# Gate and up of small expert tiles as four products at a time, behind branches of TensorE alone

## The chip, the core and the metric

One Trainium2 chip, one core of it. The time is device microseconds (us) of one execution of the whole program, and the median of 3 runs of the kernel before is 933.65 us (931.49 to 934.76). PE is TensorE, with PEld its weight loads; DVE is VectorE, ACT ScalarE, POOL GpSimd, SP SyncE, the engine that issues the weight transfers. A q behind an engine's name (PEldq) is its sequencer, which reads the instructions, takes the branches and hands work on.

## What is computed

A decoder layer for 512 tokens of width 1024: a mixer (an SSD branch and an attention branch), then a mixture of 16 experts, of which each token goes to two. The change touches the experts alone. Their part of the reference, in which `gates` is zero for all experts but the token's two:

```
for e in range(N_EXPERTS):
    hid = jax.nn.silu(t @ w_gate[e]) * (t @ w_up[e])      # 1024 -> 512, twice
    out = out + gates[:, e:e + 1] * (hid @ w_down[e])     # 512 -> 1024
```

With the inputs of the run, the router sends 31, 40, 95, 86, 27, 11, 40, 32, 91, 132, 170, 103, 25, 21, 59 and 61 tokens to the experts 0 to 15 (counted from the reference on these inputs).

## The kernel before

The mixer fills the first 560 us or so; then come the experts, then a closing layer norm. An expert's tokens are worked in tiles of H = 64: tile 0 always, tile 1 if the expert has more than 64 tokens, tile 2 if more than 128 (`tc.If(n_toks[e] > H)`, L1354, and L1356 inside it). That makes 24 tiles here: experts 2, 3, 8 and 11 have two, 9 and 10 three, the other ten one. A branch is taken by every engine for itself, from the expert's token count, which each engine loads into a register.

What a tile does, `body(e, t)`:

- `up` (L1288): gate and up, 8 steps over the width of 1024. A step is two products of 64 tokens by 512 columns; gate stands in the columns 0 to 63 of TensorE's array and up in 64 to 127, so the two run side by side. They fill one PSUM bank, gate in its upper half and up in its lower.
- `hidden` (L1292, L1293): ACT takes silu of the gate half, DVE multiplies it by the up half, into `sg`.
- `hidden_columns` (L1297, L1298): four transposes of `sg` on PE, and a copy to `hidT` by DVE.
- `down` (L1303): the product with `w_down`, from `hidT`. It is called one tile late: body(e, t) multiplies by `w_down` for the tile before it, between its own `up` and its own `hidden_columns`. `add` (L1307, L1308) then scales the result and adds it into the output rows in DRAM.
- `x_columns` (L1181, L1182) transposes the gathered tokens of the next expert; `tile_tokens` (L1156 to L1165) makes the row numbers and gates of the expert after next, and POOL gathers its tokens.

Rules of order: inside a `with in_order((PE, DVE, ACT))` block each of the three engines keeps the order in which the code is written. What lies between blocks is placed by a scheduler, which lets instructions pass a branch: before, the first products of expert e+1's `up` stand ahead of expert e's branch L1354. The weights come through a ring of 18 buffers of 1 MB, three experts deep.

A row of a four-byte product in the lists of order below is two weight loads and two products in the trace, so four instructions; a transpose is one of each.

Of the kernel before, what the change touches and what calls it, by code (L numbers as in the profile page):

```python
# [9 lines left out]
F32 = mybir.dt.float32  # L10
F32R = mybir.dt.float32r
BF16 = mybir.dt.bfloat16
I32 = mybir.dt.int32
# [4 lines left out]
P = 128  # L18
S = 512
D = 1024  # L20
NT = S // P
KT = D // P
FF = 512
NE = 16
# [4 lines left out]
UNIT = 512  # L29
EVAC = 400  # L30
DUE = 8, 4, 4
H = P // 2
INL = 3
MAXO = 10

# [72 lines left out]
def hybrid_layer(ctx: ExitStack, tc: tile.TileContext, A, out):  # L108
    nc = tc.nc

    cp = ctx.enter_context(tc.tile_pool(name="cp", bufs=1))
# [57 lines left out]
    ident = cp.tile([P, P], F32, name="ident")  # L169
# [67 lines left out]
    class Stream:  # L237
# [7 lines left out]
        def add(self, units, loads, parts):  # L245
            for n, part in enumerate(parts):
                self.parts.append((len(self.raws), n == len(parts) - 1) + part)
            self.raws.append((units, loads))
# [96 lines left out]
    class Experts:  # L345
# [18 lines left out]
        def up(self, e, k):  # L364

            assert self.nload >= 6 * e + 4
            return [self.piece(6 * e + 2 * (k // 4) + n)[:, k % 4 * FF:(k % 4 + 1) * FF] for n in range(2)]

        def down(self, e, k):
            assert self.nload >= 6 * e + 6  # L370
            return [self.piece(6 * e + 4 + k // 2)[:, k % 2 * D + n * 512:k % 2 * D + (n + 1) * 512]
                    for n in range(2)]
# [5 lines left out]
    ew = Experts([(wg_all[e], wu_all[e], wd_all[e]) for e in range(NE)], [])  # L378
# [25 lines left out]
    for j in range(4):  # L404
# [14 lines left out]
        for t, sc_ in enumerate((1, 0)):  # L419
            o = 8 * sc_ + 2 * j  # L420
# [142 lines left out]
    for g in range(4):  # L563
# [17 lines left out]
        for c in range(NT):  # L581
            nc.tensor.matmul(pt[:, c * P:(c + 1) * P], Bc.ap[:, c * P:(c + 1) * P], Cc.ap[:, c * P:(c + 1) * P],
                             start=True, stop=True)
# [14 lines left out]
        for c2 in range(2):  # L598
            pt = tr.get()
            for c in (2 * c2, 2 * c2 + 1):  # L600
                for t in range(2):
                    o = (c % 2) * 256 + t * P
# [96 lines left out]
    for j in range(4):  # L699
# [22 lines left out]
        for i in range(NT):  # L722
            w = (i + 1) * P
# [36 lines left out]
        o = FM.alloc(1)  # L760
# [81 lines left out]
    for j in range(8):  # L842
        for y in (ys[j], ya[j]):
            pt = proj(hT, KT)
            t = FM.alloc(1)
# [18 lines left out]
    def rtile(nm, shape, dt=F32):  # L864
        if dt is I32:
            return cp.tile(shape, dt, name=f"rt_{nm}")
        n = 1
        for d in shape[1:]:
            n *= d
        w = n if dt is F32 else -(-n // 2)  # L870
        a = rtc[0][:, rtc[1]:rtc[1] + w]
        if dt is not F32:
            a = a.bitcast(dt)[:, 0:n]
        rtc[1] += -(-w // 2) * 2
        for ax_ in range(len(shape) - 1, 1, -1):
            a = a.rearrange("p (a b) -> p a b", b=shape[ax_]) if ax_ == len(shape) - 1 else \
                a.rearrange("p (a b) c -> p a b c", b=shape[ax_])
        return a
# [8 lines left out]
    half = rtile("half", [P, 1])  # L887
    nc.vector.tensor_scalar(half, pcol, float(H), None, op0=ALU.is_ge)
    nc.vector.tensor_scalar(itb[:, 0:H], itf[:, 0:H], 1.0, None, op0=ALU.add)
    nc.vector.tensor_copy(itb[:, H:P], itb[:, 0:H])  # L890
    itbs = [itb] + [rtile(f"itb{t}", [P, P], BF16) for t in range(1, INL)]
    for t in range(1, INL):
        nc.vector.tensor_scalar(itbs[t], itb, float(t * H), None, op0=ALU.add)
    aux = rtile("aux", [P, NT, NE, 5], BF16)
# [82 lines left out]
    @contextmanager  # L977
    def in_order(engines):

        traced = nc.cur_bb.bb.instructions  # L980
        n, prev = len(traced), {}
        yield
        for ins in traced[n:]:
            if ins.engine in engines:
                if ins.engine in prev:
                    tc.add_manual_dep(ins, prev[ins.engine], mybir.DependencyInfo(
                        mybir.DependencyClass.NoSync, mybir.DependencyReason.DATA), reason="in_order")
                prev[ins.engine] = ins.name
# [60 lines left out]
    ET = mybir.EngineType  # L1049
# [60 lines left out]
    bgu, bys, bhid, bix = (banks[0], banks[1], banks[1]), [banks[2], banks[6]], banks[5], banks[7]  # L1110
    h2d2 = h2d.rearrange("s (h d) -> (s h) d", h=2)
    moed2 = moed.rearrange("s (h d) -> (s h) d", h=2)
    xgs, xTs, sgs, yos, ohs = {}, {}, [], [], []
# [12 lines left out]
    def setup_experts():  # L1126
# [6 lines left out]
        yos.extend(FM.alloc(1).ap for _ in range(2))  # L1133
        hidT.append(FM.alloc(1).v(4, H))
        for _ in range(3):
# [4 lines left out]
        ew.raws.append(xrc[1].ap)  # L1140
        ew.load()

    ixs = [[rtile(f"ix{e}{t}", [P, 1], I32) for t in range(INL)] for e in range(3)]
    gws = [[rtile(f"gw{e}{t}", [P, 1]) for t in range(INL)] for e in range(3)]
    ixl = [rtile(f"ixl{e}", [P, 1], I32) for e in range(2)]
    gwl = [rtile(f"gwl{e}", [P, 1]) for e in range(2)]
    rkx = rtile("rkx", [P, NT])

    def onehots(oh, ranks, slots):
# [3 lines left out]
    def tokens(oh, au, ix, gw, xg, n0=0, n1=5, at=128):  # L1153

        pi = bix[:, at + n0:at + n1]
        nc.tensor.matmul(pi, onesb, bigb[:, n0:n1], start=True, stop=False)  # L1156
        for c in range(NT):
            nc.tensor.matmul(pi, oh[:, c, :], au(c)[:, n0:n1], start=False, stop=(c == NT - 1))
        if n0 == 0:
            nc.vector.tensor_scalar(ix, bix[:, at:at + 1], bix[:, at + 1:at + 2], half, op0=ALU.add, op1=ALU.add)  # L1160
            nc.gpsimd.indirect_dma_start(out=xg, out_offset=None, in_=h2d2,  # L1161
                                         in_offset=bass.IndirectOffsetOnAxis(ap=ix[:, 0:1], axis=0),
                                         bounds_check=2 * S - 1, oob_is_err=False)
        if n1 == 5:
            nc.vector.tensor_reduce(gw, bix[:, at + 2:at + 5], axis=AX.X, op=ALU.add)  # L1165

    def oh_of(e, t):
        return ohs[t if e or t == 2 else 3 + t]

    def tile_ranks(e, t):  # L1170
        onehots(oh_of(e, t), rk[:, :, e], itbs[t])

    def tile_tokens(e, t, n0=0, n1=5):
        tokens(oh_of(e, t), lambda c: aux[:, c, e, :], ixs[e % 3][t], gws[e % 3][t], xgs[e % 2, t], n0, n1,
               128 + 8 * (e % 2 * 3 + t))

    def x_columns(xg, xT):

        pt = tr.get()
        for b in range(4):  # L1180
            nc.tensor.transpose(pt[:, b * P:(b + 1) * P], xg[:, b * P:(b + 1) * P], ident)  # L1181
        nc.scalar.copy(xT, pt)  # L1182
# [21 lines left out]

    NB = S // H - INL
    cnt = rtile("cnt", [P, 16])
    cnti = rtile("cnti", [P, 17], I32)
# [20 lines left out]
    with in_order((ET.PE, ET.DVE, ET.Activation)):  # L1228
# [46 lines left out]
        for e, t in early:  # L1275
            tile_ranks(e, t)
            tile_tokens(e, t, 0, 2)
# [7 lines left out]
    def up(strm, e, xT, bank):  # L1285
        for k in range(KT):
            for n, w in enumerate(strm.up(e, k)):
                nc.tensor.matmul(bank[n * H:(n + 1) * H], xT[:, (2 * (k % 4) + k // 4) * H:(2 * (k % 4) + k // 4 + 1) * H],  # L1288
                                 w, start=(k == 0), stop=(k == KT - 1))

    def hidden(bank, sg):
        nc.scalar.activation(sg[H:P], bank[0:H], AF.Silu)  # L1292
        nc.vector.tensor_tensor(sg[H:P], sg[H:P], bank[H:P], op=ALU.mult)  # L1293

    def hidden_columns(sg):
        for t in range(4):
            nc.tensor.transpose(bhid[:, t * P:(t + 1) * P], sg[:, t * P:(t + 1) * P], ident)  # L1297
        nc.vector.tensor_copy(hidT[0], bhid.rearrange("p (k s) -> p k s", s=P)[:, :, H:P])  # L1298

    def down(strm, e, bank):  # L1300
# [11 lines left out]
    def body(e, t):  # L1312

        bank, by, yo, sg = bgu[t], bys[t % 2], yos[t % 2], sgs[t % 2]
        with in_order((ET.PE, ET.DVE, ET.Activation)):
            if t == 0:
                if e + 2 < NE:
                    for u in range(2):
                        tile_ranks(e + 2, u)
                tile_ranks(e, 2)  # L1320
            if t == 1:
                tile_tokens(e, 2)
            up(ew, e, xTs[e % 2, t], bank)
            if e == 0 and t == 0:
                for e_, t_ in early:
                    tile_tokens(e_, t_, 2, 5)
            hidden(bank, sg)
            nc.vector.tensor_copy(ixl[e % 2], ixs[e % 3][t])
            nc.vector.tensor_copy(gwl[e % 2], gws[e % 3][t])
            if t:  # L1330
                down(ew, e, by)
                add(by, yo, ixs[e % 3][t - 1], gws[e % 3][t - 1])
            elif e:
                down(ew, e - 1, by)
                add(by, yo, ixl[1 - e % 2], gwl[1 - e % 2])
                ew.drop(2)
            if t == 0 and e + 1 < NE:
                for u in range(2):
                    x_columns(xgs[1 - e % 2, u], xTs[1 - e % 2, u])
            if t == 1:  # L1340
                x_columns(xgs[e % 2, 2], xTs[e % 2, 2])
            hidden_columns(sg)
            if t == 0 and e + 2 < NE:
                for u in range(2):
                    tile_tokens(e + 2, u)

    n_toks = [nc.values_load(cnti[0:1, e:e + 1], min_val=0, max_val=S) for e in range(NE)]  # L1347
    n_over = nc.values_load(cnti[0:1, 16:17], min_val=0, max_val=MAXO)
    n_raw = len(ew.raws)
    assert n_raw >= 18  # L1350

# [6 lines left out]
        if e + 1 < NE:  # L1358
            ew.drop(4)
    down(ew, NE - 1, bys[0])  # L1360
    add(bys[0], yos[0], ixl[(NE - 1) % 2], gwl[(NE - 1) % 2])


    spare = [ew.piece(6 * (NE - 3) + n) for n in range(18)]
# [103 lines left out]
```

## Time and profile before

| | us |
|---|---|
| median of 3 runs | 933.65 |
| profiled execution, its own time | 932.47 |
| its span in the trace | 930.6 |
| PE busy with products, of the span | 842.8 (91%) |
| DVE busy | 540.6 (58%) |
| ACT busy | 309.6 (33%) |
| gate and up (L1288), all 24 tiles, busy (570 to 900 us) | 188.3 |
| down (L1303), busy (570 to 900 us) | 97.7 |

The profile is of one execution; a duration that is read from it belongs to the 932.47 us. Two products that run side by side are counted once in the busy time. The idle time behind an instruction's row in square brackets is what its engine waited just before it, and what ended the wait.

### The profile page before, as it was taken

The numbers are of one execution on the slowest core, as the hardware profiler recorded it, in microseconds if no ns is written. First come the engines' busy times: TensorE is split into PE (matmuls) and PEld (weight loads), VectorE is DVE, ScalarE is ACT, GpSimd is POOL, SyncE is SP. The second block draws the span as 40 slices with busy tenths as digits, with TensorE's granted clock in tenths as the row PEclk, the third lists the DMA queues.
The fourth block names the chain that finished last, engine by engine and source line by source line (L and its number), as shares of the span: only waits on it lengthen the run. The fifth ranks groups of instructions, "written<-read, shape, count | busy, mean of one in ns | idle before, by whom it ended". The sixth has DMA issues, their size and how long they took to land. (4 is left out here: it accounts for less than half of the span.)

```text
span 930.6 us, 11855 instructions
## 1 busy us (share of the span) xinstructions
PE 842.8 (91%) x4216; PEld 542.3 (58%) x4216; DVE 540.6 (58%) x1310; ACT 309.6 (33%) x558; POOL 101.3 (11%) x113
## 2 busy tenths in 40 slices
PE   2899989999999999999999995999999999999850
PEld 1678768887666677878888883433343333333320
DVE  6849879858876687977745784423333223122216
ACT  5438788444643432432233451101110010001100
POOL 1001000000000000000000011122222221122210
PEclk9899999999999999999999985999999999999985
DMA  9951457213122248795445289598799998459734
GB/s 288 340 147 52 152 173 191 87 40 103 46 69 72 91 140 268 222 302 160 147 143 186 106 305 398 211 385 296 247 391 386 385 381 287 145 192 314 278 71 180
DMA packets 137170, 194.88 MB, mean 209 GB/s; under 512 B 11819, under 2 KB 85723, under 8 KB 137073
## 3 DMA queue, kind: packets, MB, share of 16 engines
q1 hardware_dynamic: 127040, 174.81, 55.3%
q0 software_dynamic: 9584, 18.45, 7.6%
q8 instruction: 46, 0.75, 0.3%
q10 hardware_dynamic: 464, 0.58, 0.2%
q14 instruction: 36, 0.29, 0.1%
HBM read 189.04 MB, written 13.16 MB: 217 GB/s over the span
## 5 line engine op out<-in xcount | busy, mean ns | idle before, releaser
L398 PE MATMUL bank<-rm,rm 128*128 128x512 f32 x512 | 206.2, 407 | 0.4 <-ACT rm L431 0.4
L400 PE MATMUL bank<-rm,rm 128*128 128x512 f32 x512 | 205.8, 402 | 0.0
L399 PE MATMUL bank<-rm,rm 128*128 128x512 f32 x512 | 204.8, 400 | 0.2 <-DVE rm L433 0.2
L1288 PE MATMUL bank<-fm,fm 128*64 128x512 f32 x408 | 123.8, 601 | 4.4 <-issue 2.0
L1288 PE MATMUL bank<-bm,fm 128*64 128x512 f32 x360 | 118.4, 597 | 1.6 <-PEq L1356 0.4
L234 DVE TENSOR_TENSOR rm<-fm,rm 128x1024 fp32r<-128x1024 f32 (+1 forms) x76 | 87.6, 1163 | 42.9 <-ACT rm L233 27.3
L398 PEld LDWEIGHTS bank<-rm,rm 128*128 128x128 f32 x512 | 97.8, 192 | 21.9 <-issue 3.1
L399 PEld LDWEIGHTS bank<-rm,rm 128*128 128x128 f32 x512 | 97.4, 190 | 21.5 <-issue 2.1
L400 PEld LDWEIGHTS bank<-rm,rm 128*128 128x128 f32 x512 | 97.1, 190 | 20.8 <-issue 2.3
L1293 DVE TENSOR_TENSOR bm<-bm,bank 64x512 f32<-64x512 f32 x24 | 16.6, 692 | 152.4 <-ACT bm L1292 143.4
L233 ACT CAST rm<-fm 128x1024 fp32r<-128x1024 f32 (+1 forms) x76 | 75.2, 1007 | 79.5 <-PE bank L399 59.5
L1292 ACT ACTIVATE bm<-bank 64x512 f32<-64x512 f32 x24 | 14.1, 588 | 198.8 <-PE bank L1288 198.8
L1288 PEld LDWEIGHTS bank<-fm,fm 128*64 128x64 f32 x408 | 37.9, 138 | 59.3 <-issue 58.4
L1303 PE MATMUL bank<-bm,fm 128*64 128x512 f32 x256 | 65.2, 593 | 0.7 <-DVEq L1354 0.7
L1288 PEld LDWEIGHTS bank<-bm,fm 128*64 128x64 f32 x360 | 34.7, 137 | 47.7 <-issue 46.8
L390 DVE SCALAR_TENSOR_TENSOR fm<-fm,cact,fm 128x256 f32<-128x256 f32 x112 | 51.2, 480 | 1.8
L1182 ACT COPY fm<-bank 128x512 f32<-128x512 f32 x38 | 20.9, 588 | 85.8 <-PE bank L1181 85.7
L1307 DVE SCALAR_TENSOR_TENSOR fm<-bank,fm,fm 128x512 f32<-128x512 f32 x24 | 18.0, 750 | 47.8 <-PE bank L1303 42.8
L1001 PE MATMUL bank<-rm,rm 128*128 128x512 f32 x192 | 44.2, 391 | 0.3 <-ACT fm L846 0.3
L1161 POOL DMA_INDIRECT bm<-h2d,rt_ix x38 | 39.0, 1027 | 38.9 <-DVE fm L1165 18.2
L1303 PEld LDWEIGHTS bank<-bm,fm 128*64 128x64 f32 x256 | 22.1, 137 | 35.3 <-issue 34.4
L1308 POOL DMA_INDIRECT moed<-fm,rt_ixl x16 | 25.5, 1596 | 152.2 <-DVE fm L1307 152.2
(314 smaller groups left out, 1101.7 us busy)
## 6 DMA issues: line engine op xcount, KB each, us to landing
bm<-in_w_down SPq DMA_DIRECT2D x22, 1024.0 KB
fm<-in_w_in SPq DMA_DIRECT2D x36, 512.0 KB
fm<-in_w_gate SPq DMA_DIRECT2D x17, 1024.0 KB
fm<-in_w_mod SPq DMA_DIRECT2D x16, 1024.0 KB
fm<-in_w_up SPq DMA_DIRECT2D x16, 1024.0 KB
bm<-in_w_up SPq DMA_DIRECT2D x16, 1024.0 KB
bm<-in_w_gate SPq DMA_DIRECT2D x15, 1024.0 KB
fm<-in_w_down SPq DMA_DIRECT2D x10, 1024.0 KB
```

Source lines behind the costliest of these rows:

```text
L233: ins = nc.scalar.copy(hi, src)
L234: nc.vector.tensor_tensor(lo, src, hi.bitcast(F32), op=ALU.subtract)
L390: nc.vector.scalar_tensor_tensor(acc, r, cact[:, k:k + 1], acc, op0=ALU.mult, op1=ALU.add)
L398: nc.tensor.matmul(pt, whi[:, k, :], ah.ap, start=(k == 0), stop=False)
L399: nc.tensor.matmul(pt, whi[:, k, :], al.ap, start=False, stop=False)
L400: nc.tensor.matmul(pt, wlo[:, k, :], ah.ap, start=False, stop=(k == nk - 1))
L1001: nc.tensor.matmul(wps[i][hf], sta.ap[:, tsl], mov.ap[:, hf * 512:(hf + 1) * 512], start=(k == 0 and sta is mh and mov is wh), stop=(k == ...
L1161: nc.gpsimd.indirect_dma_start(out=xg, out_offset=None, in_=h2d2, in_offset=bass.IndirectOffsetOnAxis(ap=ix[:, 0:1], axis=0), bounds_check ...
L1182: nc.scalar.copy(xT, pt)
L1288: nc.tensor.matmul(bank[n * H:(n + 1) * H], xT[:, (2 * (k % 4) + k // 4) * H:(2 * (k % 4) + k // 4 + 1) * H], w, start=(k == 0), stop=(k = ...
L1303: nc.tensor.matmul(bank[n * H:(n + 1) * H], hidT[0][:, k, :], w, start=(k == 0), stop=(k == 3))
L1308: nc.gpsimd.indirect_dma_start(out=moed2, in_=yo, in_offset=None, compute_op=ALU.add, out_offset=bass.IndirectOffsetOnAxis(ap=ix[:, 0:1], ...
```

## The change

`up` gets a second form for a tile with at most Q = 32 tokens: 512 columns are cut in two halves of 256, and gate and up of both halves stand in four strips of 32 columns of the array, so four products of 32 tokens by 256 columns make a step. Which form runs is decided by a branch that only PE takes, from a copy of the token count in a register of PE's own (`n_pe`, 16 of them, all loaded at the first use). `hidden` is as it was. `hidden_columns` gets a branch of the same kind: for the small tile it picks the halves apart with four products by columns of the identity. The branches stand between the blocks of kept order, so the one block of a tile becomes three. The index and gate columns of a tile (`ixs`, `gws`, `ixl`, `gwl`), which three experts or two shared in turn, get a place for every tile of every expert.

```diff
-    ixs = [[rtile(f"ix{e}{t}", [P, 1], I32) for t in range(INL)] for e in range(3)]
-    gws = [[rtile(f"gw{e}{t}", [P, 1]) for t in range(INL)] for e in range(3)]
-    ixl = [rtile(f"ixl{e}", [P, 1], I32) for e in range(2)]
-    gwl = [rtile(f"gwl{e}", [P, 1]) for e in range(2)]
+
+    ixa, gwa = cp.tile([P, NE, INL + 1], I32, name="ixa"), cp.tile([P, NE, INL + 1], F32, name="gwa")
+    ixs, gws = ([[a[:, e, t:t + 1] for t in range(INL)] for e in range(NE)] for a in (ixa, gwa))
+    ixl, gwl = ([a[:, e, INL:INL + 1] for e in range(NE)] for a in (ixa, gwa))
...
+    def up_few(strm, e, xT, bank):
+        for k in range(KT):
+            at = (2 * (k % 4) + k // 4) * H
+            for n, w in enumerate(strm.up(e, k)):
+                for hf in range(2):
+                    o = n * H + hf * Q
+                    nc.tensor.matmul(bank[o:o + Q, 0:256], xT[:, at:at + Q], w[:, hf * 256:(hf + 1) * 256],
+                                     start=(k == 0), stop=(k == KT - 1), tile_position=(0, o))
...
-    def hidden_columns(sg):
-        for t in range(4):
-            nc.tensor.transpose(bhid[:, t * P:(t + 1) * P], sg[:, t * P:(t + 1) * P], ident)
+    def hidden_columns(sg, is_few=None):
+        with ExitStack() as arms:
+            if is_few is not None:
+                with tc.If(is_few) as few:
+                    for t in range(4):
+                        o = H + t // 2 * Q
+                        nc.tensor.matmul(bhid[:, t * P + H:t * P + H + Q], sg[:, t % 2 * P:(t % 2 + 1) * P],
+                                         ident[:, o:o + Q], start=True, stop=True)
+                arms.enter_context(few.Else())
+            for t in range(4):
+                nc.tensor.transpose(bhid[:, t * P:(t + 1) * P], sg[:, t * P:(t + 1) * P], ident)
...
+        with tc.If(n_pe[e] <= t * H + Q) as few:
+            up_few(ew, e, xTs[e % 2, t], bank)
+        with few.Else():
             up(ew, e, xTs[e % 2, t], bank)
+        with in_order(engines):
...
-            hidden_columns(sg)
+        hidden_columns(sg, n_pe[e] <= t * H + Q)
+        with in_order(engines):
...
+    n_pe = [nc.values_load(cnti[0:1, e:e + 1], engines=(ET.PE,), min_val=0, max_val=S) for e in range(NE)]
```

How PE's instructions move. First place: PE, the end of tile 0 of expert 4. In the kernel before, `up` (L1288) is followed by `down` of the tile before (L1303), the transposes of the next expert's tokens (L1181) and only then by its own `hidden_columns` (L1297):

```order
L1288 MATMUL bank_61<-bm_3758,fm_81 64x512
L1288 MATMUL bank_61<-bm_3759,fm_81 64x512
L1303 MATMUL bank_63<-bm_3754,fm_74 64x512 x4
L1303 MATMUL bank_63<-bm_3755,fm_74 64x512 x4
L1181 MATMUL bank_65<-ident,bm_3751 128x128 x4
L1181 MATMUL bank_64<-ident,bm_3751 128x128 x4
L1297 MATMUL bank_66<-ident,bm_3752 128x128 x4
```

The same place in the changed kernel (L1345 is the branch around `up`, L1311 the one around `hidden_columns`, L1314 and L1318 its two arms, L1382 the branch on more than 64 tokens, which was L1354):

```order
L1288 MATMUL bank_61<-bm_3749,fm_81 64x512
L1288 MATMUL bank_61<-bm_3750,fm_81 64x512
L1345 UNCONDITIONAL_BRANCH
L1311 COMPARE_AND_BRANCH
L1314 MATMUL bank_66<-ident,bm_3743 128x32 x4
L1311 UNCONDITIONAL_BRANCH
L1318 MATMUL bank_66<-ident,bm_3743 128x128 x4
L1311 UNCONDITIONAL_BRANCH
L1374 TENSOR_LOAD rt_cnti
L1382 COMPARE_AND_BRANCH
```

`down` and the transposes of tokens no longer stand between `up` and `hidden_columns` of one tile, and the branch on the number of tiles stands right behind them. Tile 0 of each of the experts 4 to 15 has this order.

Second place: PE, where that branch lands when the expert has one tile (the end of its body, L1382). In the kernel before it lands in the rest of the next expert's `up`:

```order
L1356 UNCONDITIONAL_BRANCH x2
L1354 UNCONDITIONAL_BRANCH
L1288 MATMUL bank_61<-bm_3757,fm_81 64x512
L1288 MATMUL bank_61<-bm_3756,fm_81 64x512
L1288 MATMUL bank_61<-bm_3757,fm_81 64x512
```

In the changed kernel (L1324 is `down`):

```order
L1384 UNCONDITIONAL_BRANCH x2
L1382 UNCONDITIONAL_BRANCH
L1324 MATMUL bank_63<-bm_3745,fm_74 64x512 x4
L1324 MATMUL bank_63<-bm_3746,fm_74 64x512 x4
L1181 MATMUL bank_65<-ident,bm_3742 128x128 x4
L1181 MATMUL bank_64<-ident,bm_3742 128x128 x4
```

There `down` of the tile just transposed comes first, then the transposes of tokens, the index products and the whole of the next `up`. What the branch jumps over has grown from about 230 instructions of PE to about 530, since both forms of `up` and of `hidden_columns` lie in it.

Third place: PE, behind the first `up` of expert 0, the loads of the counts (15 of them follow one another; the first stands ahead of the branch):

```order
L1345 UNCONDITIONAL_BRANCH
L1376 ISA x2
L1376 TENSOR_LOAD rt_cnti
L1376 ISA x2
L1376 TENSOR_LOAD rt_cnti
```

In the kernel before, the index products (L1156) stand there, right behind `up`.

## Rows read from the trace of the kernel before

**Rows 1.** The page: busy time of PE; clock granted to it, in 40 slices.
```profile
PE 842.8 (91%) x4216; PEld 542.3 (58%) x4216; DVE 540.6 (58%) x1310; ACT 309.6 (33%) x558; POOL 101.3 (11%) x113
...
PEclk9899999999999999999999985999999999999985
```
**Rows 2.** Groups: instructions x count, busy us, mean ns, idle before.
```profile
L417 PE MATMUL bank<-ones,fm 128*128 128x1 f32 x32 | 5.6, 297 | 3.1 <-DVE fm L412 3.1
```
**Rows 3.** Timeline, second tile of expert 3 (start us, us, what, idle before).
```profile
653.13 0.59 PE L1288 MATMUL bank<-fm,fm 128*64 128x512 f32 x1
...
653.56 3.60 PE L1303 MATMUL bank<-bm,fm 128*64 128x512 f32 x16
...
653.84 0.59 ACT L1292 ACTIVATE bm<-bank 64x512 f32<-64x512 f32 x1 [10.23 <-PE bank L1288]
...
654.46 0.69 DVE L1293 TENSOR_TENSOR bm<-bm,bank 64x512 f32<-64x512 f32 x1 [7.33 <-ACT bm L1292]
...
657.59 0.60 PE L1297 MATMUL bank<-ident,bm 128*128 128x128 f32 x4
...
658.23 0.42 DVE L1298 COPY fm<-bank 128x256 f32<-128x256 f32 x1 [0.26 <-PE bank L1297]
...
658.61 4.93 PE L1288 MATMUL bank<-bm,fm 128*64 128x512 f32 x21 [0.42 <-PEq L1356]
```
**Rows 4.** Timeline, experts 6 and 7, one tile each.
```profile
696.07 0.60 PE L1297 MATMUL bank<-ident,bm 128*128 128x128 f32 x4
...
697.63 1.07 PE L1288 MATMUL bank<-bm,fm 128*64 128x512 f32 x2
...
698.86 6.62 PE L1288 MATMUL bank<-bm,fm 128*64 128x512 f32 x29 [0.15 <-PEq L1354]
...
710.21 0.60 PE L1297 MATMUL bank<-ident,bm 128*128 128x128 f32 x4
```
**Rows 5.** Line L1347, loads of counts: duration ns min/median/max, first and last start.
```profile
L1347 SPq TENSOR_LOAD <-rt_cnti x16: 261/262/490, 572.7 to 581.7; - x16
...
L1347 PEldq TENSOR_LOAD <-rt_cnti x16: 297/300/490, 590.8 to 891.2; - x16
```
**Rows 6.** PE's branches by line, the instruction transfers, and a row behind a branch.
```profile
L1354 PEldq COMPARE_BRANCH  x16: 70/316/452, 591.4 to 891.6; - x16
...
L1356 PEldq COMPARE_BRANCH  x12: 65/175/313, 629.7 to 839.1; - x12
...
L1421 PEldq COMPARE_BRANCH  x1: 3393/3393/3393, 895.0 to 895.0; - x1
...
q8 instruction: 46, 0.75, 0.3%
...
883.17 3.22 PE L1288 MATMUL bank<-fm,fm 128*64 128x512 f32 x14 [1.86 <-issue]
```
**Rows 7.** Stretches: length, busy us by engine, granted clock, DMA share, GB/s.
```profile
31.00:34.00 3.00, 0.83 (x4) 0.36 (x2) 2.86 (x5) 1.27 (x2) 0.00 (x0) 1.00 1.10 348
34.00:38.00 4.00, 3.14 (x13) 3.03 (x14) 2.04 (x5) 1.96 (x3) 0.00 (x0) 0.54 1.11 345
38.00:42.00 4.00, 4.00 (x12) 3.11 (x11) 3.96 (x7) 2.59 (x4) 0.00 (x0) 0.61 1.17 301
...
123.00:126.00 3.00, 0.48 (x4) 0.48 (x5) 2.17 (x4) 2.98 (x7) 0.00 (x0) 1.00 0.99 335
126.00:129.00 3.00, 3.00 (x13) 2.45 (x12) 2.98 (x9) 2.98 (x9) 0.54 (x1) 0.58 0.33 86
129.00:132.00 3.00, 3.00 (x14) 2.55 (x13) 1.31 (x3) 2.05 (x4) 0.00 (x0) 0.85 0.03 10
...
881.00:884.00 3.00, 1.14 (x5) 0.38 (x5) 0.43 (x3) 0.00 (x0) 0.00 (x0) 1.00 0.26 32
```

**Rows 8.** Timeline, end of the first tile of expert 2.
```profile
628.90 0.69 DVE L1293 TENSOR_TENSOR bm<-bm,bank 64x512 f32<-64x512 f32 x1 [7.33 <-ACT bm L1292]
...
632.03 0.60 PE L1297 MATMUL bank<-ident,bm 128*128 128x128 f32 x4
```

More of the change, by code (lines that the diff above doesn't have):

```diff
@@ L31 @@
 DUE = 8, 4, 4
-H = P // 2
+H, Q = P // 2, P // 4
 INL = 3
@@ L1173, in tile_tokens @@
     def tile_tokens(e, t, n0=0, n1=5):
-        tokens(oh_of(e, t), lambda c: aux[:, c, e, :], ixs[e % 3][t], gws[e % 3][t], xgs[e % 2, t], n0, n1,
+        tokens(oh_of(e, t), lambda c: aux[:, c, e, :], ixs[e][t], gws[e][t], xgs[e % 2, t], n0, n1,
                128 + 8 * (e % 2 * 3 + t))
@@ L1314, in body @@
         bank, by, yo, sg = bgu[t], bys[t % 2], yos[t % 2], sgs[t % 2]
-        with in_order((ET.PE, ET.DVE, ET.Activation)):
+        engines = ET.PE, ET.DVE, ET.Activation
+        with in_order(engines):
             if t == 0:
@@ L1327, in body @@
             hidden(bank, sg)
-            nc.vector.tensor_copy(ixl[e % 2], ixs[e % 3][t])
-            nc.vector.tensor_copy(gwl[e % 2], gws[e % 3][t])
+            nc.vector.tensor_copy(ixl[e], ixs[e][t])
+            nc.vector.tensor_copy(gwl[e], gws[e][t])
             if t:
                 down(ew, e, by)
-                add(by, yo, ixs[e % 3][t - 1], gws[e % 3][t - 1])
+                add(by, yo, ixs[e][t - 1], gws[e][t - 1])
             elif e:
                 down(ew, e - 1, by)
-                add(by, yo, ixl[1 - e % 2], gwl[1 - e % 2])
+                add(by, yo, ixl[e - 1], gwl[e - 1])
                 ew.drop(2)
@@ L1341, in body @@
                 x_columns(xgs[e % 2, 2], xTs[e % 2, 2])
-            hidden_columns(sg)
+        hidden_columns(sg, n_pe[e] <= t * H + Q)
+        with in_order(engines):
             if t == 0 and e + 2 < NE:
@@ L1360, in hybrid_layer @@
     down(ew, NE - 1, bys[0])
-    add(bys[0], yos[0], ixl[(NE - 1) % 2], gwl[(NE - 1) % 2])
+    add(bys[0], yos[0], ixl[NE - 1], gwl[NE - 1])
     spare = [ew.piece(6 * (NE - 3) + n) for n in range(18)]
```

## The prediction

> **What bounds the kernel now.** I read the page first, for the engine that is never idle; then the groups by line, for how often a thing occurs; then the timeline of two places in the expert stage, one inside a two-tile expert and one between one-tile experts; last the sequencer's rows and a few windows of the clock, for prices. The page has PE busy for nine tenths of every slice from the mixer to the last expert, with a high granted clock in them [rows 1]; the reader is to see that there is no stretch in which PE waits for weights for long. In the timeline of a second tile [rows 3] PE goes from `up` straight to `down` of the tile before (653.56), and ACT and DVE do silu and product beside it: `up` ends at 653.72 (653.13 + 0.59), silu starts 0.12 later, the product ends at 655.15 (654.46 + 0.69). So a chain of 1.43 us behind `up` lies under 3.60 us of `down` and is paid by nobody. Behind `hidden_columns` (657.59) PE waits 0.42 for its sequencer and goes on. Between one-tile experts [rows 4] it is the same: `hidden_columns` at 696.07, the first two products of the next `up` at 697.63, the branch costs 0.15, the rest of `up` runs, and the next `hidden_columns` starts at 710.21. A one-tile expert takes 710.21 - 696.07 = 14.14 us, nearly all of it PE. The order of PE's work is thus what hides every other engine; the change takes time from `up` and changes that order.
>
> **What it gains (A).** In [rows 4] 29 records of `up` take 6.62 us; less the last one's own 0.59 that is 14 steps in 6.03, 0.43 us per pair that runs side by side. A tile has 32 records, 16 pairs, 6.9 us. Ten tiles have at most 32 tokens (tile 0 of experts 0, 4, 5, 7, 12 and 13, the last tile of 2, 3, 8 and 9: 31, 27, 11, 32, 25, 21, 31, 22, 27 and 4). Their products are half as wide. If all four run side by side, half of 6.9 goes, 3.43 a tile, 34 in all. If the array still takes two at a time nothing goes. No row shows four. Each few tile issues 64 products and 64 weight loads where it had 32 and 32, so issue may leave a little of it; I take 3.2 us and ten tiles: -32 (bounds -34 and 0).
>
> [...]
>
> **What it costs.** *B, columns of the few tiles.* Four products of four-byte data replace four transposes in ten tiles. L417 is the nearest product by ones: 32 records, 16 products, 5.6 us [rows 2], 0.35 each against 0.60 / 4 = 0.15 for a transpose [rows 3]. The difference of 0.2 x 4 x 10 would be 8; the products are only 32 columns wide, and L417 is one column. I take +4, and +3 to +10 as bounds.
>
> *C, fifteen loads of `n_pe` behind the first `up`.* One load of a count is 0.30 us on PE's sequencer; sixteen on SP's start 9.0 us apart from first to last, 0.6 a piece [rows 5]. Nothing of PE's stands between them, and the index products of expert 0 are behind. 15 x 0.6 = 9, less about 1 of products still queued: +8 (bounds +3.5 from 15 x 0.3 less 1, and +9).
>
> *D, silu and product.* From expert 4 on `hidden_columns` of tile 0 follows its own `up` at once, as the order shows. The 1.43 us of [rows 3] have no cover then, and some 0.1 goes by until PE starts: 1.5 x 12 experts = +18 (bounds +14, if part of the records' modelled end is not there, and +21). What loses the cover is not what is late next: `down` and the transposes are not removed, only moved ahead of `up`.
>
> *E, the branch behind `hidden_columns`.* It is now followed at once by `down` of the same tile, which needs `hidT`, that is 0.60 of `hidden_columns`, then DVE's copy of 0.42 that starts 0.04 behind them [rows 3]. Before, products of the next `up` were there. In the same chain PE's sequencer loads the count (0.30, [rows 5]) and takes the branch. L1354 jumps over some 230 instructions and is 0.32 us in the median, 0.45 at most; L1421 jumps over some 1,270 and took 3.39 [rows 6]. The 530 of the changed kernel lie between. The trace has 46 transfers of instructions of 16 KB each (0.75 MB) [rows 6]; PE's program has some 12,400 instructions, so a transfer holds about 270 of them, and 530 are two of these. A jump of 230 mostly lands in the piece being read or in the next, one of 530 behind both. So I price it by the far row: 0.3 + 3.39 + 0.3 (the branch's landing and first weight load, like the 0.15 to 0.42 idle in [rows 3, 4]) = 4.0 us from `hidden_columns` to `down`, in place of 0.44 + 0.15 to 0.42. That is some 3.2 us more in the eight one-tile experts from 4 on (4, 5, 6, 7, 12, 13, 14, 15); expert 0 loses 3.3, since only its branch moves, and expert 1 about 1, having products beside it: 25.6 + 4.3 = +30. If the branch stays at 0.32, the chain over DVE sets it, and some 0.6 x 8 = +5 is left (bounds +5 and +34).
>
> That row on L1421 agrees with the Trainium skill, "Runtime: NRT & Kernel Launch", section "Instruction fetch mechanics": a taken branch whose target is outside the two pages held must have that page brought first, and a page holds 256 instructions. By that rule 530 always leave the pages, and by the row this is 3.39 us; the rule is what speaks against the cheap end.
>
> *F, the rest.* 24 pairs of branches around `up` and `hidden_columns`, all PE's own, at 0.07 us least [rows 6]; most are read while products queue before them. 24 x 2 x 0.07 = 3.4: +3 (bounds 0 and +8, with 0.175 each). The columns with a place of their own change no instruction's size; they take away waits on readers two or three experts back, which the rows don't have: 0.
>
> *G, the clock.* E and D leave PE with 1.5 us of waiting, 0.6 of work, then 3.5 of waiting. In [rows 7] PE is busy for 0.83 of 3 us up to 34, and for 4 + 4 us after it the granted clock is 0.54 and 0.61, near the 1.2 GHz level; it is busy for 0.48 of 3 us up to 126, and 0.58 and 0.85 follow. At these clocks (1 - 0.54) x 4 + (1 - 0.61) x 4 = 3.4 us and (1 - 0.58) x 3 + (1 - 0.85) x 3 = 1.7 us of full-speed work are lost, 2.55 in the mean. Against it: a wait of 1.86 us at 883.17 [rows 6], with 1.14 us of work in its 3 us, left the clock at 1.00 in them. The place in question has less work than that in 5.6 us, so I take 2.55 x 8 = +20 (bounds 0 and 27).
>
> **The sum.** -32 + 4 + 8 + 18 + 30 + 3 + 20 = +51. On the profiled execution (span 930.6 and 1.9 around it, 932.5) that is 983.5; the median stands 1.2 above it. I take 983. What is given back: nothing I see, as weights run three experts ahead and a slower PE needs them later.
>
> **The rivals.**
> 1. *The fetch comes but the clock holds.* G is 0: 932.5 + 31 = 963 (955 to 970). For it the row at 883.17; against it the two windows of [rows 7].
> 2. *The jump stays short.* The branch stays near 0.32 us, since what is jumped is mostly read by then. E is 5, G 0 or little: -32 + 4 + 8 + 18 + 5 + 3 = +6, 938 (930 to 950). For it: the waits of L1354 in [rows 4], 0.15 us. Against it L1421.
> 3. *Faster: the sequencer runs on past waiting products.* If PE's loads and branches are handled while earlier products wait in its queue, then C, E and F go under D's wait and under `up`, and so do the branch waits of before (0.15 to 0.42 in [rows 3, 4], eight times: -2). For it: the first compare of L1356 stands at 629.7 [rows 6], 2.3 us before the products ahead of it start at 632.03 [rows 8], so the sequencer can be far ahead. Against it: 629.7 is 0.1 after 629.59, where the DVE product for which those products wait is done [rows 8]; it may have waited just there, and then it passes nothing in the changed order. -34 + 4 + 5.6 (C at bounds' middle) + 18 + 5 - 2 = -3.4: 929 (925 to 931).
> 4. *Four products do not run four at a time.* For it: no row has more than two side by side. Against it: two do, at 0.43 us a pair [rows 4]. A is 0 and all else stays: 932.5 + 51 + 32 = 1015 (995 to 1020; the low end with a rate between two and four).
>
> **How the numbers follow.** Forecast 0.46 (983, own range 970 to 1000), rival 1 0.18, rival 2 0.18, rival 3 0.10, rival 4 0.08. Two executions of this kernel differ by about 0.3%, 2.8 us, and less than this I call the same. Rival 3 is faster on the whole (0.10), with 0.02 from the low end of rival 2; the same is 0.06, from rival 2; all else is slower, 0.82. The range drops most of rival 3 and the far part of rival 4: 934 to 1003.
>
> **What would show it.** PE's busy time of the few `up` at half of 6.9 us in a tile of 27 tokens (A); a block of 15 L1376 loads on PEq, 0.6 us apart near 591 (C); 1.5 us idle before `hidden_columns` released by DVE L1293 in experts 4 to 15 (D); L1382 branches of about 3.4 us in the experts with one tile, with a transfer of instructions beside each (E); a granted clock near 0.5 to 0.6 behind them (G). A median L1382 of 0.3 makes E wrong, a clock of 1.00 there G, a few `up` of 6.9 us A. If the span is below 931 the order of instructions is not what decides, and rival 3 was right.

## The result, and the profile after

The changed kernel takes 1014.75 us (median of 4, 1012.77 to 1015.77) against 934.2 us before: a ratio of 1.0865 (95% interval 1.0836 to 1.0894), 81 us slower. The forecast was 983 us with a range of 934 to 1003; the direction and every term of its sum are there, but the sum is 32 us too small. The profiled execution has a span of 1013.6 us, 83.0 more than before.

From the page of the changed kernel: busy time, granted clock in 40 slices, and the transfers of instructions (count, MB, share).

```profile
PE 839.7 (83%) x4576; PEld 550.0 (54%) x4576; DVE 540.0 (53%) x1310; ACT 309.7 (31%) x558; POOL 101.3 (10%) x113
...
PEclk9999999999999999999998579787788999997875
...
q8 instruction: 73, 1.20, 0.5%
```

Against [rows 1] PE is busy for 3 us less over a span 83 us longer, so it is idle for 86 us more. Its busy time hides two changes that nearly cancel: the few `up` are shorter, and the clock is below full speed through most of the expert stage, which makes products longer. Instruction transfers went from 46 [rows 6] to 73.

What PE waited for, changed kernel: us in total, times, longest.

```profile
PE bank L1324 <- PEq L1382: 49.1, 10, 6.2
PE bank L1318 <- DVE bm L1306: 13.1, 9, 2.0
PE bank L1181 <- DMA bm<-h2d,ixa: 10.5, 4, 5.4
PE bank L1156 <- issue: 9.5, 1, 9.5
...
PE bank L1314 <- DVE bm L1306: 7.2, 5, 1.4
...
PE bank L1324 <- PEq L1384: 5.6, 2, 3.0
```

L1324 is `down`, L1382 the branch on more than 64 tokens, L1384 that on more than 128; L1314 and L1318 are the two forms of `hidden_columns`, L1306 DVE's product, L1181 the transposes of tokens, L1156 the first index product behind the 15 loads of `n_pe`. The first line alone is six tenths of the loss.

One cycle of a one-tile expert with few tokens (expert 4) in the changed kernel's timeline, the counterpart of [rows 3] and [rows 4]:

```profile
690.68 3.66 PE L1301 MATMUL bank<-bm,fm 128*32 128x256 f32 x64
...
694.41 0.59 ACT L1305 ACTIVATE bm<-bank 64x512 f32<-64x512 f32 x1 [14.05 <-PE bank L1301]
...
695.03 0.69 DVE L1306 TENSOR_TENSOR bm<-bm,bank 64x512 f32<-64x512 f32 x1 [3.07 <-ACT bm L1305]
...
695.77 1.08 PE L1314 MATMUL bank<-ident,bm 128*128 128x32 f32 x8 [1.43 <-DVE bm L1306]
...
702.86 6.30 PE L1324 MATMUL bank<-bm,fm 128*64 128x512 f32 x16 [6.01 <-PEq L1382]
```

The four products do run four at a time: `up` takes 3.66 us where it took 7.85 (697.63 to 705.48, [rows 4]). Before, the busy time of the whole stage gives the same 7.85 for a tile (188.3 / 24). Then come 1.43 us of waiting for silu and product, 1.08 for `hidden_columns`, 6.01 for the branch, and a `down` of 6.30 us that took 3.60 [rows 3]. Why 6.30 is in the windows of the same stretch (columns as in [rows 7]):

```profile
690.00:694.00 4.00, 3.52 (x69) 2.16 (x68) 1.92 (x12) 0.00 (x0) 2.05 (x2) 1.00 1.04 393
694.00:698.00 4.00, 1.42 (x16) 0.97 (x8) 2.08 (x5) 1.66 (x3) 0.97 (x1) 1.00 1.06 389
698.00:702.00 4.00, 0.00 (x0) 0.00 (x0) 0.00 (x0) 0.00 (x0) 0.63 (x1) 0.50 1.02 393
702.00:706.00 4.00, 3.14 (x8) 1.12 (x10) 0.74 (x4) 0.00 (x0) 0.00 (x0) 0.50 0.76 228
706.00:710.00 4.00, 4.00 (x18) 1.71 (x15) 0.00 (x0) 0.00 (x0) 0.00 (x0) 0.72 1.04 395
```

PE does nothing from 698 to 702, the granted clock goes to 0.50 (1.2 GHz), and `down` runs through most of its time at that level.

The sum term by term, in us of the profiled execution:

| term | forecast | measured | from |
|---|---|---|---|
| A, few `up` | -32 | -42 | 10 x (3.66 - 7.85) |
| B, few columns | +4 | +5 | 10 x (1.08 - 0.60) |
| C, `n_pe` loads | +8 | +9.5 | wait of L1156 |
| D, silu and product | +18 | +20 | 13.1 + 7.2 |
| E, the long jump | +30 | +50 | 49.1 + 5.6 + 1.1 behind L1345, less 6 behind branches before |
| F, other branches | +3 | about +2 | rest of the waits of L1324 |
| G, clock | +20 | +35 | busy time x (1 - clock) in windows of 2 us: 37.3 against 2.4 |
| gathered tokens late | 0 | +5 | 10.5, of which 5.4 stood before |
| sum | +51 | +84.5 | span: +83.0 |

### The profile page after: what moved, and what is told of

Read it like the earlier page. It is cut to its first block, busy times and chain, and to the rows that moved or that the text cites. A ratio compares the mean times of both kernels' runs of the same rounds, so it can differ in the third digit from the quotient of the medians.

```text
span 1013.6 us, 12683 instructions
## 1 busy us (share of the span) xinstructions
PE 839.7 (83%) x4576; PEld 550.0 (54%) x4576; DVE 540.0 (53%) x1310; ACT 309.7 (31%) x558; POOL 101.3 (10%) x113
## 5 line engine op out<-in xcount | busy, mean ns | idle before, releaser
L1324 PE MATMUL bank<-bm,fm 128*64 128x512 f32 x256 | 76.8, 755 | 43.7 <-PEq L1382 39.6
L1151 DVE TENSOR_SCALAR fm<-fm 128x128 bf16<-128x128 bf16 x192 | 36.4, 265 | 118.3 <-PE bank L1158 75.3
L1288 PE MATMUL bank<-fm,fm 128*64 128x512 f32 x240 | 73.0, 616 | 1.6 <-issue 1.5
L1324 PEld LDWEIGHTS bank<-bm,fm 128*64 128x64 f32 x256 | 23.4, 173 | 85.3 <-issue 80.7
L1288 PE MATMUL bank<-bm,fm 128*64 128x512 f32 x208 | 65.9, 609 | 1.5 <-issue 0.9
L1306 DVE TENSOR_TENSOR bm<-bm,bank 64x512 f32<-64x512 f32 x24 | 16.6, 691 | 89.0 <-ACT bm L1305 76.3
L1161 POOL DMA_INDIRECT bm<-h2d,ixa x38 | 39.1, 1028 | 203.4 <-DVE fm L1151 151.0
L1329 POOL DMA_INDIRECT moed<-fm,ixa x24 | 38.3, 1598 | 146.5 <-DVE fm L1328 124.8
L1324 PE MATMUL bank<-fm,fm 128*64 128x512 f32 x128 | 37.7, 717 | 13.3 <-PEq L1382 9.5
L1288 PEld LDWEIGHTS bank<-fm,fm 128*64 128x64 f32 x240 | 23.2, 142 | 36.2 <-issue 36.1
```

The costliest lines, as they stand in the source:

```text
L1151: nc.vector.tensor_scalar(oh[:, c, :], slots, ranks[:, c:c + 1], None, op0=ALU.is_equal)
L1324: nc.tensor.matmul(bank[n * H:(n + 1) * H], hidT[0][:, k, :], w, start=(k == 0), stop=(k == 3))
L1329: nc.gpsimd.indirect_dma_start(out=moed2, in_=yo, in_offset=None, compute_op=ALU.add, out_offset=bass.IndirectOffsetOnAxis(ap=ix[:, 0:1], ...
```

## The experiments

What had to be told apart after this: theory 1, that the length of the jump and the lost cover each cost what the table says; its rivals, that the order alone makes the branch long, or that what is jumped doesn't matter. Then, why a jump took 6 us and not 3.4.

**1. The order of before kept around the branches.** The two branches go inside the block of kept order.

```
-        with tc.If(n_pe[e] <= t * H + Q) as few:       # between two blocks
+            with tc.If(n_pe[e] <= t * H + Q) as few:   # inside one block, hidden_columns too
```

> The changed kernel with its three blocks of kept order made one again, the two branches inside it: PE has down of the tile before and the transposes of tokens between up and hidden_columns once more, everything else (four products, loads, jump over some 530 instructions) stays. Theory 1 (long jump and lost cover each cost, and add): the 17 us of waits for silu and product go, some 10 us of the waits behind L1382 are covered by index products, and half of the lost clock comes back: 970 to 985. Rival (the jump costs only because hidden_columns and down stand on both sides of it): 935 to 950.

996.95 us, 18 us less than the changed kernel and 12 to 27 more than expected. The waits for DVE's product are gone, the long branches are not, and no more of them is covered. Of the 35 us of clock only 9.5 come back, not half (27.8 us in the measure of term G). One of the branches in its timeline, and one line of its waits:

```profile
703.25 0.64 PE L1301 MATMUL bank<-bm,fm 128*32 128x256 f32 x2 [6.59 <-PEq L1380]
```
```profile
PE bank L1288 <- issue: 23.8, 3, 11.1
```

The rival falls: the jump does not need `down` behind it to cost. It stops whatever follows, here the next `up`, and one wait of 11.1 us holds the long branch (6.09 us at 758.21) and the next one's, around `up` (4.48 us at 764.51).

**2. The two forms in tile 0 alone**, tiles 1 and 2 as before, so that the jump has 231 instructions of PE again.

```
-            body(e, 1)
+            body_plain(e, 1)      # one block, plain up; body_plain(e, 2) too
```

> The changed kernel with the two forms of up and of hidden_columns in tile 0 alone; tiles 1 and 2 are written as in the kernel before, so the jump over them has some 230 instructions again. Four of the ten few tiles are lost, 13 us of gain. Theory 1 (the length of the jump makes the long branches): waits behind L1382 fall from some 50 to under 10 us, the lost clock from 24 to under 10, time 950 to 968. Rival (a branch behind hidden_columns is long whatever it jumps over): 1000 to 1030, branches of 3 to 6 us as before.

971.31 us (966.81 to 975.68). The order is the changed one, the branch is short again. First the changed kernel, then this one:

```profile
L1382 PEldq COMPARE_BRANCH  x16: 77/3876/6278, 605.8 to 971.8; - x16
```
```profile
L1417 PEldq COMPARE_BRANCH  x16: 77/277/917, 611.8 to 937.0; - x16
```

The median is 0.28 us against 3.88, and PE waits 1.4 us behind this branch in place of 49.1. The length decides, not the place behind `hidden_columns`. The time is 3 us above the expected range. The clock loses 22.9 us in the measure of term G, where under 10 was expected. The wait for gathered tokens is 11.0 us, about as in the changed kernel (10.5).

**3. The few tiles by hand**, no branch, no `n_pe`, the order of before (it holds for these counts alone).

```
+    FEW = {(0, 0), (2, 1), (3, 1), (4, 0), (5, 0), (7, 0), (8, 1), (9, 2), (12, 0), (13, 0)}
...
+            (up_few if (e, t) in FEW else up)(ew, e, xTs[e % 2, t], bank)
```

> The kernel before with the ten few tiles written out by hand in the new forms of up and hidden_columns, by expert and tile, with no branch, no n_pe and the order of before (valid for these counts alone). Theory 1 (the products gain 33 us and the hidden columns give 5 back): 934 - 28 = 906 (902 to 911). Rival (weights bind once PE is faster): 915 or more, with PE waiting for DMA.

925.3 us, a ratio of 0.9919 (0.9895 to 0.9943): 8 us faster, not 28. The products gain what they should, 34 us of busy time at equal clock; 12 us of it go to the clock (busy time x (1 - clock): 14.6 against 2.4) and 13 to new waits, among them stops inside `up` itself:

```profile
699.89 0.65 PE L1301 MATMUL bank<-bm,fm 128*32 128x256 f32 x4 [3.37 <-issue]
```

This wait stands behind 41 of the 64 records, not behind 32, where the next buffer of weights begins, and it ends 1.2 us after a transfer of instructions has landed (698.67 in the trace). So the rival of weights that bind falls too. That PE waits for its program is read from these times: the second such wait (2.83 us, until 849.33) ends 1.3 us after a transfer of instructions, and the 1.86 of [rows 6] 1.4 us after one. The two waits inside `up` make 6.2 of the 13 us.

**4. The order alone.** `down` of the tile before and the transposes of tokens ahead of `up` in experts 4 to 15, in the kernel before.

```
+            if t == 0 and e >= 4:
+                down(ew, e - 1, by)
+                add(by, yo, ixl[1 - e % 2], gwl[1 - e % 2])
+                ...                                   # x_columns too
             up(ew, e, xTs[e % 2, t], bank)
```

> The kernel before with down of the tile before and the transposes of tokens written ahead of up in tile 0 of experts 4 to 15, as the changed kernel has them on PE; nothing else is changed, the jump has some 230 instructions. Theory 1: 12 waits of 1.4 us for silu and product, 8 of some 0.7 us for the copy to hidT, and a few us of clock: 955 to 968. Rival (DVE and ACT hide it, order is harmless): under 940.

979.68 us, 46 us slower, 12 more than the top of the range. Two lines of its waits and one of its timeline:

```profile
PE bank L1181 <- DMA bm<-h2d,rt_ix: 19.2, 11, 5.3
PE bank L1297 <- DVE bm L1293: 17.0, 12, 1.4
```
```profile
701.21 1.09 PE L1181 MATMUL bank<-ident,bm 128*128 128x128 f32 x4 [3.89 <-DMA bm<-h2d,rt_ix]
```

The 17.0 is term D, forecast as 18. The 19.2 I had not seen: the transposes, moved ahead of `up`, come some 8 us earlier in the order and now wait for the tokens that POOL gathers (13.8 beyond the 5.4 that stand before). With 16 us of clock (18.7 against 2.4) that is the 46, to 1 us. In the changed kernel only 5 us of the late tokens show. That its long jumps give the gather this time is likely but not shown: experiment 2 has the same order with short jumps, and its wait is 11.0 us, not 19.2.

**5 and 6. Jumps of many lengths, in the order of before.** Products that never run are put where the one-tile expert jumps.

```
+            if PADS[e]:
+                with tc.If(n_toks[e] > 500):
+                    for n in range(PADS[e]):
+                        nc.tensor.matmul(bgu[2][0:H], ident[:, 0:H], ew.down(e, n % 4)[n // 4 % 2], start=True, stop=True)
```

> The kernel before with products that never run (behind a branch on more than 500 tokens) put at the end of what a one-tile expert's branch L1354 jumps over: 16, 32, 48, 64, 80 products of four instructions in experts 1, 4, 5, 6, 7 and 16, 32, 48, 64 in 12 to 15, so jumps of some 300, 360, 430, 490 and 550 instructions in the place of 230. Theory 1 (a jump past the piece of program behind the one being read costs a transfer): branches of 0.3 to 0.5 us up to some 300 instructions, of 3 us and more from some 500 on, in between by where the pieces' borders lie; time 15 to 30 us above before. Rival (long branches come from the order, not the length): all stay below 0.5 us, time within 3 us of before.

> As the last, with the lengths dealt otherwise: 48 and 32 products in experts 0 and 1, 64, 32, 16, 48 in 4 to 7, 80, 64, 32, 16 in 12 to 15. Theory 1: the same prices by length, whatever the expert. If some branches of one length take 6 us and others 3, the place of the branch in its piece of the program decides, and not the length alone.

986.0 and 971.8 us, one run each, 52 and 37 us above the kernel before, where 15 to 30 was expected. Their branch, first kernel and then second:

```profile
L1355 PEldq COMPARE_BRANCH  x16: 70/3602/6582, 591.5 to 941.4; - x16
```
```profile
L1355 PEldq COMPARE_BRANCH  x16: 70/408/6762, 590.7 to 931.0; - x16
```

By length, both kernels and the one before, experts with one tile:

| instructions jumped | branch, us |
|---|---|
| 231 (before, ten) | 0.22 to 0.45 |
| some 300 | 0.40, 0.42, 3.53, 5.42 |
| some 363 | 0.32, 0.44, 6.20, 6.50, 6.76 |
| some 427 | 3.67, 3.69, 6.03, 6.28 |
| some 491 | 5.00, 6.16, 6.16, 6.58 |
| 555 | 6.36, 6.40 |

The step is where the forecast put it, between 230 and 530, and nothing lies between 0.5 and 3.5. The rival falls. Jumps of one length (some 300, some 363) come out short and long, so the place counts beside the length, and the expectation that some 300 stays short failed in two of four. And the price of a jump is 3.5 to 6.8 us, not 3.4, and 52 us for nine of them under the order of before.

The Trainium skill, "Runtime: NRT & Kernel Launch", section "Instruction fetch mechanics", has pages of 256 instructions of which two are held. Counted so, with one starting place of the first page for all, fitted to these branches, 39 of 40 branches (ten each of before, changed and these two) come out as the rule says: landing in the same or the next page under 0.5 us, further on 3.4 and more.

**7. Both repairs at once**: kept order, tile 0 alone, and `n_pe` loaded one expert ahead.

```
+            if e + 1 < NE:
+                load_n_pe(e + 1)          # in kept order, ahead of hidden_columns
```

> Both repairs at once: the order of before kept around the branches, the two forms in tile 0 alone (six of the ten few tiles), and n_pe of an expert loaded one expert ahead, between the transposes of tokens and hidden_columns. From the few tiles by hand (8 us faster than before, some 10 us of it gone in waits for instructions and in clock): 6 tenths of that, less 16 loads of which some 0.3 us may show each: 927 to 935. Rival (branches and loads cost what the products bring): 936 to 945.

964.07 us, a ratio of 1.0332 (1.0312 to 1.0353): the rival, and worse than it. PE is busy for 9 us less than before and idle for 38 more in the stage. The two largest lines of its waits:

```profile
PE bank L1156 <- DVE gwa L1165: 18.0, 20, 1.5
PE bank L1288 <- issue: 13.5, 3, 6.6
```

The index products (L1156) wait for DVE, 18.0 us where all their waits in the stage before come to 8.1; nothing here had priced that, and why it grew was not tested. Two waits of over 6 us stand behind a branch around `up` itself (L1385, 5.6 us each), the likely reason, not tested, being that several jumps in one expert reach program not yet there. And nine times 0.7 to 1.2 us are lost right ahead of `up`, 0.15 to 0.42 before; that no product of it stands ahead of the branches any more, as [rows 4] had it at 697.63, is the likely reason. No version with these branches beat the kernel before.

**8. Work in front of the jump.** Eight products that nobody reads between `hidden_columns` and the branch (L1386 there), 3.4 us at full clock.

```
+            if t == 0 and e >= 4:
+                for k in range(4, 8):
+                    for n, w in enumerate(ew.up(e, k)):
+                        nc.tensor.matmul(bgu[2][n * H:(n + 1) * H], ident[:, 0:H], w, start=True, stop=True)
```

> The changed kernel with eight products of 64x512 whose result nobody reads, put in experts 4 to 15 between hidden_columns (or the index products behind it) and the branch L1382, 3.4 us of PE work while its sequencer fetches. Theory 1 (PE's clock falls because PE is idle in the fetch, and the products behind it run at half speed): down behind a jump returns from 6.3 to some 3.6 us, the clock behind it to above 0.8; if the products run beside the fetch the time falls by 15 to 25 us, to 990 to 1000; if the sequencer reaches the branch only when they have run, it rises by 10 to 25 us, 1025 to 1040, with the clock up all the same. Rival (the clock does not depend on it): down stays at 6 us.

1020.57 us, between the two cases. Expert 4 in its timeline, and the window of its `down`:

```profile
697.61 5.35 PE L1376 MATMUL bank<-bm,ident 128*64 128x512 f32 x16
...
704.48 3.65 PE L1324 MATMUL bank<-bm,fm 128*64 128x512 f32 x16 [1.51 <-PEq L1386]
```
```profile
703.00:706.00 3.00, 1.52 (x8) 0.74 (x10) 0.74 (x4) 0.00 (x0) 0.00 (x0) 1.00 0.36 71
```

`down` is back at 3.65 us and the clock at 1.00, and so is `down` in the experts 5, 6, 7 and 14. In the experts 12 and 13 the products end 3.2 and 3.3 us before `down` can start, and `down` takes 5.35 us (6.55 and 6.50 in the changed kernel):

```profile
925.65 5.35 PE L1324 MATMUL bank<-bm,fm 128*64 128x512 f32 x16 [3.19 <-PEq L1386]
```

So the half speed does come from PE's idle time in the jump. The branch itself stays at 6.1 us, but most of it now lies beside products. From the end of `hidden_columns` to that of `down` it is 11.5 us in place of 12.3 in expert 4. From the `hidden_columns` of one expert's tile 0 to that of the next, the experts 4 to 7 and 12 to 14 take 5.9 us less in sum, and the experts 8 to 11, which have more tiles and no long jump to fill, 12.3 us more. That is the +6 measured.

**9 and 10. The weights not loaded.** The loads for experts 3 to 15 are left out (these are computed with the weights of experts 0 to 2), in the changed kernel and in the one before.

```
+                if self.nload < 18:
                     nc.sync.dma_start(self.piece(self.nload).rearrange("p (a b) -> p a b", b=n), src)
```

> The changed kernel with the loads of gate, up and down of the experts 3 to 15 left out (these are computed with the weights of the experts 0 to 2 that are still in the ring), so that the DMA engines are nearly idle from some 640 us on. Nothing of PE's program changes. Theory 1b (a jump past the program held costs one transfer of instructions, and that transfer queues behind the weights' packets): every branch L1382 falls to 3.3 to 4.2 us, those of 6.0 to 6.3 us in the experts 4, 5, 7, 12 and 13 above all; time 985 to 1000. Rival (6 us comes from the short form of up or from where the branch stands in its piece of the program): the same five stay at 6 us, 1008 to 1016.

> The same loads left out of the kernel before, as the measure for the last run. PE seldom waits for weights there and its branch does not leave the program held: 930 to 934 by theory 1b; much under 930 would mean that weights held the kernel before back too.

Branches of the changed kernel with the DMA engines quiet:

```profile
L1383 PEldq COMPARE_BRANCH  x16: 77/3368/5106, 607.7 to 888.8; - x16
```

The five of 6.0 to 6.3 us (experts 4, 5, 7, 12 and 13) are 3.3, 3.3, 3.4, 4.0 and 4.0; the one of 5.1 is expert 15's, at a DMA share of 0.59. That part of the expectation holds but for expert 15. In these experts it isn't the load alone that differs: without the loads the scheduler put the next expert's `up` ahead of L1383, so that PE's program did change, against what I had written. The clean case is expert 1, up to whose jump, and over it, PE has the same instructions in both kernels. Its branch goes from 5.96 to 3.79 us. The stretches in which it starts, in the changed kernel and without the loads:

```profile
621.00:625.00 4.00, 4.00 (x22) 1.78 (x19) 0.00 (x0) 0.00 (x0) 0.00 (x0) 1.00 1.06 361
```
```profile
623.00:627.00 4.00, 4.00 (x24) 1.71 (x20) 0.00 (x0) 0.00 (x0) 0.00 (x0) 1.00 0.17 26
```

The times are no price of the jump: 932.35 us there (985 to 1000 was expected) and 923.82 for the kernel before. The latter is 10 us under its usual time, more than expected: its waits for index columns shrink by 6 us, and those of 2.4 us inside `up` go.

**11. The counts one expert ahead** in the changed kernel.

> The changed kernel with n_pe of an expert loaded one expert ahead, behind the transposes of its tokens, where the changed kernel loads all at the first use. Theory 1: the 9.5 us wait behind the first up goes, each later load shows with at most 0.3 us: 1004 to 1010. Rival (loads cost the same wherever they stand): 1012 to 1016.

1004.16 us: 10.6 less, the whole of term C and a little of the clock behind it. The wait of 9.5 us at L1156 is gone.

**12. More loads instead of fewer**, with the order on PE, DVE, ACT and POOL word for word as in the changed kernel.

```
-    ew = Experts([(wg_all[e], wu_all[e], wd_all[e]) for e in range(NE)], [])
+    ew = Experts([(wg_all[e], wu_all[e], wd_all[e]) for e in (*range(NE), 0, 1)], [])
```

> The changed kernel with twelve more loads of 1 MB behind those of expert 15 (weights of the experts 0 and 1 into buffers that have come free, read by nobody), so that the DMA engines are busy while the experts 14 and 15 are worked, which they were not. The order on PE, DVE, ACT and POOL is the same, word for word. Theory 1b (the transfer of instructions queues behind the weights): the branches L1382 of the experts 14 and 15 rise from 3.39 and 3.91 us to between 5.5 and 6.5 us, those of all other experts stay within 0.3 us. Rival (the place in the program or the form of up decides): they stay at 3.4 and 3.9 us.

`down` behind the jumps of experts 14 and 15, and the DMA share (last but one column) while they were waited for, in the changed kernel and then with the added loads (the second row of each pair ends with the stretch that was asked for; the wait in brackets is what counts here):

```profile
958.07 5.00 PE L1324 MATMUL bank<-fm,fm 128*64 128x512 f32 x16 [3.47 <-PEq L1382]
...
975.98 1.98 PE L1324 MATMUL bank<-bm,fm 128*64 128x512 f32 x4 [3.98 <-PEq L1382]
```
```profile
954.00:958.00 4.00, 0.60 (x4) 0.36 (x4) 1.32 (x5) 0.27 (x1) 1.59 (x1) 0.93 0.12 13
971.00:975.00 4.00, 0.66 (x4) 0.42 (x4) 1.58 (x5) 1.28 (x1) 1.57 (x1) 0.93 0.14 12
```
```profile
953.06 6.07 PE L1324 MATMUL bank<-fm,fm 128*64 128x512 f32 x16 [4.71 <-PEq L1382]
...
973.28 3.68 PE L1324 MATMUL bank<-bm,fm 128*64 128x512 f32 x8 [5.23 <-PEq L1382]
```
```profile
948.00:952.00 4.00, 0.34 (x4) 0.10 (x1) 0.99 (x2) 0.01 (x1) 1.59 (x1) 0.89 0.70 232
967.00:971.00 4.00, 0.66 (x4) 0.42 (x4) 1.64 (x5) 1.28 (x1) 1.57 (x1) 1.00 1.08 385
```

The branches went from 3.39 to 4.64 and from 3.91 to 5.16 us; all others stayed within 0.25. Both stay below the 5.5 to 6.5 us that were expected, with the first of the two at a share of 0.70 only, but nothing other than the loads differs, so the load makes the jump dearer. The same is seen inside the changed kernel, where the experts differ in nothing but form and neighbours:

```profile
745.13 5.65 PE L1324 MATMUL bank<-bm,fm 128*64 128x512 f32 x16 [4.20 <-PEq L1382]
...
917.41 6.55 PE L1324 MATMUL bank<-bm,fm 128*64 128x512 f32 x16 [6.22 <-PEq L1382]
```
```profile
740.00:744.00 4.00, 0.66 (x4) 0.42 (x4) 1.52 (x5) 0.60 (x2) 1.61 (x1) 0.80 0.71 260
...
910.00:914.00 4.00, 1.08 (x8) 0.97 (x8) 1.45 (x5) 0.43 (x1) 1.62 (x1) 0.88 1.06 387
```

A wait of 3.5 and 4.0 us at a DMA share of 0.12 and 0.14, 4.2 at 0.71, 6.2 at 1.06: the fuller the DMA engines, the longer the jump. In the changed kernel's trace the transfer of instructions that a jump needs starts 1.0 to 1.6 us after the branch when the engines are quiet and 3.5 to 3.8 us after it when they are full. It takes about 1 us in both, and each of the ten branches ends 1.3 to 1.5 us after it has landed.

## Why the forecast was wrong

- *What bounds the kernel, and the order as cover:* right. D was 20 us against 18, and 17.0 by itself in experiment 4.
- *A:* the mechanism right, the size too small (-42 for -32): I halved the 6.9 us of steps and took off for issue, but a few `up` also saves the tail and the wait inside the old one (7.85 to 3.66). Rival 4 named 1015 us and met the time by accident; its mechanism, products not four at a time, is wrong.
- *B, C, F:* right within 2 us each.
- *E is the step that failed.* "So I price it by the far row": 3.39 us of L1421 was read where the weights had all been fetched; the DMA share is 0.26 between that branch and its transfer. A long jump waits for a transfer, and six of the ten stand where the DMA engines are full (shares of 1.03 to 1.06), a seventh at 0.71. The waits of the ten are 49.1 us, where 4.0 x 8 and the smaller shares of experts 0 and 1 gave 36. These 13 us are most of what E lacks; the rest is the jumps inside the experts with more tiles (L1384: 5.6, L1345: 1.1), which had no price at all. Experiment 12, expert 1 in experiment 9 and the rows of 740 and 910 show the load to be the cause of 6 in place of 3.4.
- *G:* the mechanism right (experiment 8), the size too small. 2.55 us were taken for eight places. But `down`, 3.65 us at full clock, takes 6.0 to 6.6 us in the experts 4, 5, 7, 12 and 13 with waits of 6 us, and 5.0 to 6.3 in the four with waits of 3.5 to 4.3, and what follows it is slow too. The gap of term C costs some (the clock is 0.55 in the ten us behind 590).
- *"What is given back: nothing I see":* wrong by 5 us here and by 14 in experiment 4. `x_columns` was moved past 7 us of `up`, and what it waits for, POOL's gather, was not asked for.
- Rivals 1 to 3 fall: the clock did not hold, the jump did not stay short, and the sequencer did not run past products that wait for another engine. In expert 4 the compare of L1382 starts at 696.45, 0.68 us after `hidden_columns` has begun (695.77) and so behind its wait for DVE. Past products that run it does go, as experiment 8 shows.
- Two slips in the working change nothing here. The middle of C's bounds, used in rival 3, is 6.25 and not 5.6, and G counts the whole 4 us from 34 to 38 where PE was busy for 3.14.

Left open: why one jump at a full share takes 3.53 us (expert 1 in experiment 5) and others at the same share take 6, and why the transfer starts later under load; that it stands in line behind weights is a guess. No run here looks into the queue.

## What to carry to other kernels

Count the instructions that a branch jumps over before adding a second form of anything inside its body: code that never runs is not free when the jump over it leads out of the part of the program that has been fetched, and two forms of one step more than doubled this jump. Price such a jump from a place with the same DMA traffic, and ask for it at every branch, not only at the one you look at. When an instruction is moved earlier, ask of each of its inputs when it arrives, not only what it used to cover.

## What the hardware showed that I had not expected

- A long branch takes more than half as long again under DMA traffic: 3.4 to 3.9 us at a DMA share under 0.3, 6.0 to 6.3 at 1.0 in the changed kernel.
- Even where no branch is added a faster `up` seems to run out of program: waits of 3.37 and 2.83 us inside it, each until 1.2 to 1.3 us after a transfer of instructions (experiment 3). With these, other waits and the clock, 8 us are left of the 34 that four products at a time gain there.
- PE can work beside a jump, if products stand in its queue: with eight of them the 6.1 us branch left 1.51 us of idle time (experiment 8, expert 4).
